# A two-layer fp32 decoder trunk on one core: x loaded ahead of the second weight strip, squares last, gated high parts queued behind the PSUM copies

## The chip, the cores and the metric

The kernel runs on one core of a Trainium2 chip, in one launch. The metric is the device time of that launch in microseconds (us). The kernel before was timed three times: 1942.38, 1941.19 and 1939.77 us, median 1941.19. One further execution was recorded by the profiler.

Engines are named as the profile names them: PE is TensorE (PEld its weight loads), DVE is VectorE, ACT is ScalarE, POOL is GpSimd, SP is the engine whose queue issues most transfers.

## The reference

The trunk works on a residual stream of 512 tokens by 1024 features in float32. It has two layers, each a half feed-forward, a mixer and another half feed-forward, so there are four feed-forward blocks, called ffn 0 to 3 here. The mixers (an mLSTM, a sparse attention) are not touched by the change.

```python
def rmsnorm(x, g):
    y = xf * lax.rsqrt(jnp.mean(xf * xf, axis=-1, keepdims=True) + EPS)
    return y * g

def swiglu(h, w_in, w_out):
    a, b = jnp.split(h @ w_in, 2, axis=-1)        # w_in: 1024 x 5632
    return (jax.nn.silu(a) * b) @ w_out           # w_out: 2816 x 1024

    h = h + 0.5 * swiglu(rmsnorm(h, ffn_norm[layer, 0]), ...)
```

## The kernel before

**Number format.** Every matrix product is made of three matmuls. An operand is cut into a high part (the value rounded to a shorter format) and a low part (value minus high part). ACT writes the high part with a copy, DVE subtracts it from the value and writes the low part. PE multiplies high by high, low by high and high by low into the same PSUM tile (`mm3`). Tile names tell which is which: `xhi`, `xlo` are the parts of the activations, `whi`, `wlo` of the weights, `thi`, `tlo` of sums of activations, `ghi`, `glo` of the gated hidden values.

**Layout.** The residual stream is held transposed, as eight tiles `h` of 128 features by 512 tokens. Weights come as strips of 128 output features, 512 KB each, through raw tiles `wraw` (two buffers), and are cut into `whi`, `wlo` (four buffers each). A strip against all of x is 8 times 3 matmuls of 512 columns.

**The start.** `setup` issues the loads on SP's queue: the first tile of x, the gains, three more tiles of x, the second weight strip as one 512 KB transfer (`load_weight`), the last four tiles of x, constants. The first strip was issued from ACT's queue in two halves (`load_first`). `norm_in` then makes the parts of x (ACT `xhi` line 289, DVE `xlo` line 290) and the sum of squares over the features: ACT squares a tile (lines 297 and 300), and POOL (tiles 1 to 3) or DVE (tiles 5 to 7) adds it to one of two sums `ssq` (line 301). The first two strips (p = 0) go through `plain`, which interleaves them: the second strip starts when the first has gone over four tiles of x. The next two strips (p = 1) follow. In them `rstd_columns` multiplies the sum of squares by a column of ones on PE and DVE computes the reciprocal root; `rstd_rows` later spreads it over the partitions with two matmuls from `rd`.

**A feed-forward block.** The 22 blocks of hidden features are taken in three thirds (`EVENS`: 8, 8 and 6 blocks). For a pair of blocks the gate half (weight block p) and the linear half (block 22 + p) are made, both mostly by `by_seven`: a two-by-two block product in seven instead of eight products, 84 matmuls of 256 columns. Its weights are quarters `q` and sums of quarters `s`, in four groups. The products land in three PSUM tiles A, Z and B. ACT copies quarters of them to SBUF in this order: A (into `fw`), the right half of Z (into `fu`), B (into `fu`), the rest of A (into `fw`), all on line 481. The fifth product writes the left half of Z, and is made to wait until ACT has copied Z's right half. After a gate half, `silu` multiplies by the reciprocal root on DVE (line 406) and applies SiLU on ACT (line 408). After a linear half, `gate` multiplies the two on DVE (line 415), and `split` writes `ghi` on ACT (line 245) and `glo` on DVE (line 246). At the end of a third, the gated blocks go through the out-projection. ffn 2 uses another variant (`by_seven_apart`).

**What sets the order.** A list scheduler merges the traced instructions into one queue for each engine. The engines work their queues strictly in order: an instruction that waits holds all that stand behind it on its engine.

Of the kernel before, what the change touches and what calls it, by code (L numbers as in the profile page):

```python
# [100 lines left out]
class Net:  # L101
# [38 lines left out]

    def load_weight(self):
# [107 lines left out]
    def setup(self):  # L249
# [6 lines left out]
        self.rest = lambda: None  # L256
# [20 lines left out]
    def norm_in(self, gcol, ssq=True, loaded=False):  # L277
# [7 lines left out]
        def parts(b):  # L285
            hi = self.xp.tile([P, T], F32R, name="xhi", tag="xhi")
            lo = self.xp.tile([P, T], F32R, name="xlo", tag="xlo")
            g = self.g[:, gcol + b:gcol + b + 1]
            nc.scalar.activation(hi, self.h[b], AF.Copy, scale=g)
            t = nc.vector.scalar_tensor_tensor(lo, self.h[b], g, hi.bitcast(F32), op0=ALU.mult, op1=ALU.subtract)  # L290
            self.part_made = t.ins
            x.append((hi, lo))

        def squares(b):
# [3 lines left out]
            else:  # L298
                sq = self.sp.tile([P, T], F32, name="sq", tag="sq", bufs=2)
                nc.scalar.activation(sq, self.h[b], AF.Square)  # L300
                (nc.gpsimd if b < 4 else nc.vector).tensor_tensor(t, t, sq, op=ALU.add)
# [7 lines left out]
        if ssq and loaded:  # L309
            for b in range(KB):  # L310
                squares(b)
# [65 lines left out]
    def ffn(self, i, given=None):  # L377
# [7 lines left out]
        with ExitStack() as ctx:  # L385
# [17 lines left out]
            def silu(pa):  # L403
# [4 lines left out]
                nc.scalar.activation(t, pa, AF.Silu)  # L408
                return t

            def gate(t, u):
# [5 lines left out]
                hi = gp.tile([P, T], F32R, name="ghi", tag="ghi", bufs=bufs)  # L417
                lo = gp.tile([P, T], F32R, name="glo", tag="glo", bufs=bufs)
                self.split(t, hi, lo)
                gs.append((hi, lo))  # L420
# [4 lines left out]
            def x_forms(k):  # L425
# [6 lines left out]
                nc.scalar.activation(one[:, :T], self.h[k], AF.Copy, scale=g1)  # L432
# [40 lines left out]
            def by_seven(p):  # L473
# [19 lines left out]
                out(u1[:, r], A[:, l])  # L493
# [48 lines left out]
            def plain(p):  # L542
# [7 lines left out]
                if p == 0:  # L550
                    order.sort(key=lambda o: o[0] + 3.5 * o[1])
# [22 lines left out]
            for k0, k1 in EVENS if seven else LATER:  # L574
# [5 lines left out]
                for p in range(k0, k1, 2) if seven or k0 else range(k0, k1):  # L580
                    if p and (seven or k0):
                        if p in units:
                            ts = [silu(t) for t in (yield from by_seven(p))]
                        else:
                            ts = []
                            for j in range(2):
# [12 lines left out]
                                ts.append(silu(pa))  # L599
                        for t, u in zip(ts, (yield from by_seven(FB + p))):  # L600
                            gate(t, u)
# [898 lines left out]
```

## Time and profile before

| what | value |
|---|---|
| median of 3 timed runs | 1941.19 us (1939.77 to 1942.38) |
| the profiled execution, its own time | 1940.4 us |
| its span, first to last instruction | 1938.6 us |
| mean granted clock of TensorE | 0.998 |
| POOL busy | 168.1 us (9% of the span) |
| bytes read from HBM | 177.10 MB, 92 GB/s over the span |

The span is the time from the first to the last instruction of the profiled execution; the 1.8 us to its own time lie outside. The other views used below are the timeline (start, duration, engine, line, operation, and in brackets the idle time before it with what ended it), the table of waits (who waited for whom: total, times, longest), and tables of time windows (busy time of each engine with the number of instructions, the clock granted to TensorE, and what the transfers moved).

### The profile page before, as it was taken

The numbers are of one execution on the slowest core, as the hardware profiler recorded it, in microseconds if no ns is written. First come the engines' busy times: TensorE is split into PE (matmuls) and PEld (weight loads), VectorE is DVE, ScalarE is ACT, GpSimd is POOL, SyncE is SP. The second block draws the span as 40 slices with busy tenths as digits, with TensorE's granted clock in tenths as the row PEclk, the third lists the DMA queues.
The fourth block names the chain that finished last, engine by engine and source line by source line (L and its number), as shares of the span: only waits on it lengthen the run. The fifth ranks groups of instructions, "written<-read, shape, count | busy, mean of one in ns | idle before, by whom it ended". The sixth has DMA issues, their size and how long they took to land. (4 is left out here: it accounts for less than half of the span.)

```text
span 1938.6 us, 31636 instructions
## 1 busy us (share of the span) xinstructions
PE 1913.0 (99%) x11946; PEld 1693.3 (87%) x11946; DVE 1567.4 (81%) x2947; ACT 1024.9 (53%) x1979; POOL 168.1 (9%) x222
## 2 busy tenths in 40 slices
PE   9999999999999999999999999999999999999999
PEld 7989898788878999898888989898877788999897
DVE  8969788757889879697676979696899989879695
ACT  6536345445656446265354535354777766445262
POOL 0000001012200000001100000001444410000000
PEclk9999999999999999999999999999999999999999
DMA  5333322323132323323343332323322222323322
GB/s 192 115 98 104 120 83 71 116 82 96 66 126 82 122 86 104 103 72 116 117 129 107 115 113 101 103 66 113 107 66 55 66 100 86 120 88 105 101 74 93
DMA packets 81945, 192.80 MB, mean 99 GB/s; under 512 B 9920, under 2 KB 10944, under 8 KB 81792
## 3 DMA queue, kind: packets, MB, share of 16 engines
q1 hardware_dynamic: 80272, 187.76, 30.3%
q8 instruction: 94, 1.54, 0.3%
q0 software_dynamic: 512, 1.31, 0.3%
q10 hardware_dynamic: 1008, 1.70, 0.2%
q14 instruction: 59, 0.48, 0.1%
HBM read 177.10 MB, written 2.10 MB: 92 GB/s over the span
## 5 line engine op out<-in xcount | busy, mean ns | idle before, releaser
L236 PE MATMUL pmm<-xhi,whi 128*128 128x256 f32 (+1 forms) x1376 | 441.4, 321 | 6.7 <-ACT fu L481 6.1
L236 PE MATMUL pmm<-xhi,wlo 128*128 128x256 f32 (+1 forms) x1376 | 437.5, 318 | 0.4 <-DVE wlo L170 0.4
L236 PE MATMUL pmm<-xlo,whi 128*128 128x256 f32 (+1 forms) x1376 | 437.0, 318 | 0.8 <-DVE xlo L290 0.8
L167 ACT ACTIVATE whi<-wraw 128x512 fp32r<-128x512 f32 (+3 forms) x258 | 204.8, 810 | 269.6 <-PE pmm L236 163.2
L236 PE MATMUL pmm<-thi,whi 128*128 128x256 f32 x1184 | 328.8, 278 | 2.4 <-ACT fw L516 2.0
L236 PE MATMUL pmm<-thi,wlo 128*128 128x256 f32 x1184 | 327.5, 277 | 1.4 <-DVE wlo L246 1.4
L236 PE MATMUL pmm<-tlo,whi 128*128 128x256 f32 x1184 | 327.7, 277 | 0.0
L170 DVE TENSOR_TENSOR wlo<-wraw,whi 128x512 fp32r<-128x512 f32 (+3 forms) x258 | 240.3, 944 | 70.6 <-ACT whi L167 67.8
L236 PEld LDWEIGHTS pmm<-xhi,whi 128*128 128x128 f32 x1376 | 258.4, 188 | 26.2 <-ACT fu L481 7.7
L236 PEld LDWEIGHTS pmm<-xhi,wlo 128*128 128x128 f32 x1376 | 258.4, 188 | 20.1 <-DVE wlo L170 0.7
L236 PEld LDWEIGHTS pmm<-xlo,whi 128*128 128x128 f32 x1376 | 258.6, 188 | 19.8 <-DVE xlo L290 2.6
L245 ACT ACTIVATE whi<-q 128x512 fp32r<-128x512 f32 x260 | 163.9, 631 | 209.1 <-PE pmm L236 156.1
L236 PE MATMUL pmm<-glo,whi 128*128 128x512 f32 x704 | 274.4, 390 | 0.0
L236 PE MATMUL pmm<-ghi,whi 128*128 128x512 f32 x704 | 274.2, 389 | 0.0
L236 PE MATMUL pmm<-ghi,wlo 128*128 128x512 f32 x704 | 273.9, 389 | 0.0
L236 PEld LDWEIGHTS pmm<-thi,whi 128*128 128x128 f32 x1184 | 223.2, 189 | 4.0 <-ACT fw L516 3.3
L236 PEld LDWEIGHTS pmm<-thi,wlo 128*128 128x128 f32 x1184 | 223.0, 188 | 1.6 <-DVE wlo L246 1.6
L236 PEld LDWEIGHTS pmm<-tlo,whi 128*128 128x128 f32 x1184 | 223.4, 189 | 0.0
L246 DVE TENSOR_TENSOR wlo<-q,whi 128x512 fp32r<-128x512 f32 x260 | 178.0, 685 | 16.4 <-ACT whi L245 16.4
L245 ACT ACTIVATE whi<-s 128x512 fp32r<-128x512 f32 x222 | 138.5, 624 | 54.6 <-PE pmm L236 32.7
L236 PEld LDWEIGHTS pmm<-glo,whi 128*128 128x128 f32 x704 | 132.2, 188 | 28.0 <-DVE glo L246 1.1
L236 PEld LDWEIGHTS pmm<-ghi,wlo 128*128 128x128 f32 x704 | 132.2, 188 | 27.6
(380 smaller groups left out, 3246.7 us busy)
## 6 DMA issues: line engine op xcount, KB each, us to landing
q<-in_ffn_in SPq DMA_DIRECT2D x260, 256.0 KB, 2.6
wraw<-in_ffn_out SPq DMA_DIRECT2D x48, 512.0 KB, 3.5
wraw<-in_ffn_out SPq DMA_DIRECT2D x48, 384.0 KB, 3.1
wraw<-in_ffn_in SPq DMA_DIRECT2D x27, 512.0 KB, 3.8
e<-in_ffn_in SPq DMA_DIRECT2D x36, 256.0 KB, 2.7
wraw<-in_m_qk SPq DMA_DIRECT2D x8, 512.0 KB, 3.6
wraw<-in_m_v SPq DMA_DIRECT2D x8, 512.0 KB, 3.6
wraw<-in_m_og SPq DMA_DIRECT2D x8, 512.0 KB, 3.6
```

The lines of the kernel that those rows point to most:

```text
L167: t = nc.scalar.activation(hi[:p, c], raw[:p, c], AF.Copy)
L170: nc.vector.tensor_tensor(lo[:p, c], raw[:p, c], hi[:p, c].bitcast(F32), op=ALU.subtract)
L236: self.nc.tensor.matmul(out, lhsT, rhs, start=start, stop=stop, skip_group_check=shared)
L245: self.nc.scalar.activation(hi, src, AF.Copy)
L246: self.nc.vector.tensor_tensor(lo, src, hi.bitcast(F32), op=ALU.subtract)
```

## The change

The changed kernel computes the same. It moves work on three engines in the start and in ffn 0, 1 and 3.

1. **Loads.** All eight tiles of x are issued ahead of the second strip, which is now loaded in two halves of 256 KB and cut into parts half by half (`load_second`). Its parts are traced after all parts of x.
2. **First product.** In ffn 0 the first strip goes over all eight tiles of x, and then the second strip does.
3. **Squares.** In ffn 0 all eight squares and their additions stand behind the parts of x and of the second strip on ACT and DVE, and all additions are on DVE.
4. **Parked parts.** In `by_seven` blocks of ffn 0, 1 and 3, SiLU and the split of the gated values are kept back, and traced behind the last of the next block's four PSUM copies (or, at a third's end, after the last block).

```diff
+    def load_second(self):
...
+        halves = slice(0, 512), slice(512, 1024)
+        for j, c in enumerate(halves):
+            nc.sync.dma_start(v(raw)[:, 4 * j:4 * j + 4], ap[:, 4 * j:4 * j + 4])
+        self.ready.append(((name, idx), (v(hi), v(lo))))
+        def parts():
+            for c in halves:
+                a = nc.scalar.activation(hi[:, c], raw[:, c], AF.Copy)
+                d = nc.vector.tensor_tensor(lo[:, c], raw[:, c], hi[:, c].bitcast(F32), op=ALU.subtract)
+            self.last = a.ins, d.ins
+        self.second = parts
...
         for b in range(KB):
             nc.sync.dma_start(self.h[b], a["xT"][b * P:(b + 1) * P, :])
...
-            if b == 3 and self.order:
-                self.load_weight()
+        if self.order:
+            self.load_second()
...
-                (nc.gpsimd if b < 4 else nc.vector).tensor_tensor(t, t, sq, op=ALU.add)
+                (nc.vector if b >= 4 or loaded else nc.gpsimd).tensor_tensor(t, t, sq, op=ALU.add)
...
         if ssq and loaded:
-            for b in range(KB):
-                squares(b)
+            self.second()
+            self.high_made, self.part_made = self.last
+            with self.tc.issue_after(self.high_made), self.tc.issue_after(self.part_made):
+                for b in range(KB):
+                    squares(b)
...
+            parked = deque()
+            def unpark():
+                while parked:
+                    parked.popleft()()
...
-                nc.scalar.activation(t, pa, AF.Silu)
+                if park:
+                    parked.append(lambda: nc.scalar.activation(t, t, AF.Silu))
+                else:
+                    nc.scalar.activation(t, pa, AF.Silu)
...
-                self.split(t, hi, lo)
-                gs.append((hi, lo))
+                def parts():
...
+                    self.split(t, hi, lo)
+                    gs.append((hi, lo))
+                if park:
+                    parked.append(parts)
+                else:
+                    parts()
...
                 yield from product(A[:, l], s2, -2, False)
-                out(u1[:, r], A[:, l])
+                with tc.issue_after(out(u1[:, r], A[:, l]).ins):
+                    unpark()
...
-                    order.sort(key=lambda o: o[0] + 3.5 * o[1])
+                    order.sort(key=lambda o: o[0] + (3.5 if i else 7.5) * o[1])
...
-                            ts = [silu(t) for t in (yield from by_seven(p))]
+                            ts = [silu(t, seven) for t in (yield from by_seven(p))]
...
-                            gate(t, u)
+                            gate(t, u, seven)
...
+                unpark()
                 n = k1 - k0
```

The next three places show queues as they were and as they are. A row has the line of its own kernel, the operation, what it writes and reads, and the size.

On ACT in the start, before, from the fourth tile of x on: squares (`ssq`, `sq`) and the second strip (`whi`, 1024 columns) stand between the parts of x.

```order
L289 ACTIVATE xhi<-h_73,gains 128x512
L297 ACTIVATE ssq_133<-h_70 128x512
L300 ACTIVATE sq<-h_71 128x512
L167 ACTIVATE whi<-wraw 128x1024
L289 ACTIVATE xhi<-h_74,gains 128x512
L289 ACTIVATE xhi<-h_75,gains 128x512
L300 ACTIVATE sq<-h_72 128x512
L289 ACTIVATE xhi<-h_76,gains 128x512
L289 ACTIVATE xhi<-h_77,gains 128x512
L300 ACTIVATE sq<-h_73 128x512
L297 ACTIVATE ssq_134<-h_74 128x512
L300 ACTIVATE sq<-h_75 128x512
```

The same queue in the changed kernel, from the last tile of x to the third and fourth strips (the last row, `whi` of 1024 columns, twice).

```order
L313 ACTIVATE xhi<-h_77,gains 128x512
L158 ACTIVATE whi<-wraw 128x512 x2
L321 ACTIVATE ssq_132<-h_70 128x512
L324 ACTIVATE sq<-h_71 128x512
L324 ACTIVATE sq<-h_72 128x512
L321 ACTIVATE ssq_133<-h_74 128x512
L324 ACTIVATE sq<-h_73 128x512
L324 ACTIVATE sq<-h_75 128x512
L476 ACTIVATE fw<-h_70,gains 128x512
L324 ACTIVATE sq<-h_76 128x512
L324 ACTIVATE sq<-h_77 128x512
L190 ACTIVATE whi<-wraw 128x1024 x2
```

All squares now stand between the second strip's parts and the third strip's.

On DVE in the start, before, from the second strip's low part to the third and fourth strips' (the last row): three additions of squares (`ssq`), the other three being POOL's.

```order
L170 TENSOR_TENSOR wlo<-wraw,whi 128x1024
L290 SCALAR_TENSOR_TENSOR xlo<-h_74,gains,xhi 128x512
L290 SCALAR_TENSOR_TENSOR xlo<-h_75,gains,xhi 128x512
L290 SCALAR_TENSOR_TENSOR xlo<-h_76,gains,xhi 128x512
L290 SCALAR_TENSOR_TENSOR xlo<-h_77,gains,xhi 128x512
L301 TENSOR_TENSOR ssq_134<-ssq_134,sq 128x512 x2
L197 TENSOR_TENSOR s_210<-q_194,q_196 128x512
L301 TENSOR_TENSOR ssq_134<-ssq_134,sq 128x512
L198 TENSOR_TENSOR s_211<-s_210,q_190 128x512
L313 TENSOR_TENSOR ssq_134<-ssq_134,ssq_133 128x512
L199 TENSOR_TENSOR q_194<-q_190,q_194 128x512
L170 TENSOR_TENSOR wlo<-wraw,whi 128x1024 x2
```

The same queue in the changed kernel, from the last tile of x to the low part of the fourth strip.

```order
L314 SCALAR_TENSOR_TENSOR xlo<-h_77,gains,xhi 128x512
L159 TENSOR_TENSOR wlo<-wraw,whi 128x512 x2
L325 TENSOR_TENSOR ssq_132<-ssq_132,sq 128x512 x3
L325 TENSOR_TENSOR ssq_133<-ssq_133,sq 128x512
L220 TENSOR_TENSOR s_213<-q_197,q_199 128x512
L325 TENSOR_TENSOR ssq_133<-ssq_133,sq 128x512
L221 TENSOR_TENSOR s_214<-s_213,q_193 128x512
L325 TENSOR_TENSOR ssq_133<-ssq_133,sq 128x512
L193 TENSOR_TENSOR wlo<-wraw,whi 128x1024
L340 TENSOR_TENSOR ssq_133<-ssq_133,ssq_132 128x512
L193 TENSOR_TENSOR wlo<-wraw,whi 128x1024
```

Six additions now stand between the second strip's low part and the third strip's, which has moved ahead of the last sum and of one sum of quarters.

On ACT in ffn 0, second third, at the gate half of block 14, before: the four PSUM copies are the rows with `pmm`; the two `ghi` are the gated values of blocks 12 and 13.

```order
L481 ACTIVATE fw<-pmm 128x256
L245 ACTIVATE ghi<-ft 128x512
L245 ACTIVATE whi<-q_2224 128x512
L245 ACTIVATE ghi<-ft 128x512
L481 ACTIVATE fu<-pmm 128x256
L245 ACTIVATE whi<-s_2359 128x512
L481 ACTIVATE fu<-pmm 128x256
L245 ACTIVATE whi<-q_2230 128x512
L481 ACTIVATE fw<-pmm 128x256
```

The same place in the changed kernel.

```order
L525 ACTIVATE fw<-pmm 128x256
L268 ACTIVATE whi<-q_2225 128x512
L525 ACTIVATE fu<-pmm 128x256
L268 ACTIVATE whi<-s_2354 128x512
L525 ACTIVATE fu<-pmm 128x256
L268 ACTIVATE whi<-q_2231 128x512
L525 ACTIVATE fw<-pmm 128x256
L268 ACTIVATE ghi<-ft 128x512 x2
L268 ACTIVATE whi<-s_2355 128x512
```

The two `ghi` have moved from behind the first copy to behind the fourth, and stand ahead of the high parts of later weights.

More of the change, by code (lines that the diff above doesn't have):

```diff
@@ L139, in load_first @@
         self.rest = lambda: self.split(raw[:, b], hi[:, b], lo[:, b])
+    def load_second(self):
+        nc = self.nc
+        name, idx = self.order.popleft()
+        ap = self.a[name][idx]
+        raw = self.wp.tile([P, 1024], F32, name="wraw", tag="wraw", bufs=2)
+        hi = self.part("whi")
+        lo = self.part("wlo")
+        v = lambda t: t.rearrange("p (n m) -> p n m", m=P)
+        halves = slice(0, 512), slice(512, 1024)
[8 more added lines that the diff above has]
+        self.second = parts
     def load_weight(self):
@@ L255, in setup @@
         nc.vector.memset(self.ones, 1.0)
-        self.rest = lambda: None
+        self.rest = self.second = lambda: None
+        self.last = None, None
         for b in range(KB):
@@ L288, in parts @@
             g = self.g[:, gcol + b:gcol + b + 1]
-            nc.scalar.activation(hi, self.h[b], AF.Copy, scale=g)
+            self.high_made = nc.scalar.activation(hi, self.h[b], AF.Copy, scale=g).ins
             t = nc.vector.scalar_tensor_tensor(lo, self.h[b], g, hi.bitcast(F32), op0=ALU.mult, op1=ALU.subtract)
@@ L407, in silu, with gate @@
                     pa = t
-                nc.scalar.activation(t, pa, AF.Silu)
+                if park:
+                    parked.append(lambda: nc.scalar.activation(t, t, AF.Silu))
+                else:
+                    nc.scalar.activation(t, pa, AF.Silu)
                 return t
-            def gate(t, u):
+            def gate(t, u, park=False):
                 if seven and not fold:
@@ L416, in gate @@
                 bufs = 8 if seven or not k0 else 6
-                hi = gp.tile([P, T], F32R, name="ghi", tag="ghi", bufs=bufs)
-                lo = gp.tile([P, T], F32R, name="glo", tag="glo", bufs=bufs)
-                self.split(t, hi, lo)
-                gs.append((hi, lo))
+                def parts():
+                    hi = gp.tile([P, T], F32R, name="ghi", tag="ghi", bufs=bufs)
+                    lo = gp.tile([P, T], F32R, name="glo", tag="glo", bufs=bufs)
+                    self.split(t, hi, lo)
[4 more added lines that the diff above has]
+                    parts()
             def gate_plain(pa, pb):
@@ L431, in x_forms @@
                 h2, c = self.h[k + 4], [two[:, N * j:N * j + N] for j in range(3)]
-                nc.scalar.activation(one[:, :T], self.h[k], AF.Copy, scale=g1)
+                with tc.issue_after(self.high_made):
+                    nc.scalar.activation(one[:, :T], self.h[k], AF.Copy, scale=g1)
                 with tc.issue_after(self.part_made):
```

4 lines of the change are left out of this document (2 added, 2 removed).

## The prediction, made before the changed kernel was run

> **What bounds the kernel now.** I read the page first, for the engine that bounds it.
>
> ```profile
> span 1938.6 us, 31636 instructions
> PE 1913.0 (99%) x11946; PEld 1693.3 (87%) x11946; DVE 1567.4 (81%) x2947; ACT 1024.9 (53%) x1979; POOL 168.1 (9%) x222
> ```
>
> PE is busy for 99% of the span, and the change removes no matmul. So the gain can only come from PE's idle time, 25.6 us by this row, and from time in which PE runs slowly. The table of waits says where PE's queue stands longest.
>
> ```profile
> PEld pmm L236 <- ACT fu L481: 7.7, 8, 2.2
> ```
>
> The first weight load after a wait is held 8 times, 7.7 us in all, by a PSUM copy (`fu`, line 481) on ACT. All lie in ffn 0, 1 and 3. The timeline shows one of them: block 14 of ffn 0.
>
> ```profile
> 195.56 0.38 ACT L481 ACTIVATE fw<-pmm 128x256 f32<-128x256 f32 x1 [0.78 <-PE pmm L236]
> 198.71 0.63 ACT L245 ACTIVATE ghi<-ft 128x512 fp32r<-128x512 f32 x1 [2.77 <-DVE ft L415]
> 200.29 0.36 ACT L481 ACTIVATE fu<-pmm 128x256 f32<-128x256 f32 x1
> ...
> 196.79 0.68 DVE L246 TENSOR_TENSOR wlo<-s,whi 128x512 fp32r<-128x512 f32 x1
> 198.60 0.68 DVE L415 TENSOR_TENSOR ft<-ft,fu 128x512 f32<-128x512 f32 x1
> 199.80 1.31 DVE L246 TENSOR_TENSOR glo<-ft,ghi 128x512 fp32r<-128x512 f32 x2
> ...
> 199.32 0.28 PE L236 MATMUL pmm<-thi,wlo 128*128 128x256 f32 x1
> 200.70 0.38 PE L236 MATMUL pmm<-xhi,whi 128*128 128x256 f32 x1 [1.10 <-ACT fu L481]
> 200.93 0.28 PE L236 MATMUL pmm<-xlo,whi 128*128 128x256 f32 x1
> 201.04 0.28 PE L236 MATMUL pmm<-xhi,wlo 128*128 128x256 f32 x1
> ```
>
> ACT has nothing wrong with its speed. Its first `ghi` stands for 2.77 us until DVE has multiplied the gate (line 415), and the copy that PE needs is queued behind it. The matmul that could have gone at 199.43 (199.32 plus the normal distance 0.11) goes at 200.70, 1.27 us late, and the next follows at a distance of 0.23 instead of 0.11: each such wait costs another 0.11.
>
> The second kind of loss is seen in a table of windows.
>
> ```profile
> 1080.07:1083.49 3.42, 1.76 (x12) 1.55 (x13) 3.42 (x7) 3.25 (x7) 0.00 (x0) 1.00 0.25 77
> 1083.49:1086.90 3.41, 3.41 (x18) 3.41 (x17) 3.41 (x6) 1.26 (x2) 0.00 (x0) 0.50 0.53 169
> 1783.22:1786.63 3.41, 1.48 (x13) 1.48 (x13) 3.41 (x6) 3.41 (x9) 0.00 (x0) 1.00 0.24 87
> 1786.63:1790.05 3.42, 3.42 (x19) 3.42 (x18) 3.42 (x7) 1.37 (x4) 0.00 (x0) 0.50 0.45 150
> ```
>
> Columns: length, busy time of PE, PEld, DVE, ACT, POOL, granted clock, share and rate of the transfers. Twice PE was busy for only half of a stretch of 3.41 us, and both times the next 3.41 us ran at clock 0.50, which costs 1.7 us each. The second follows the longest of the eight waits (2.2 us, in ffn 3); the first is in ffn 2, which the change leaves alone.
>
> **The change in the blocks (parked parts).** The new queue has both `ghi` behind the fourth copy. In the example the copies then wait only for PE's own products. What hides the parked work: the `ghi` are needed by the out-projection, which for this pair comes more than a block later, and the third's last pair is unparked at once. What is late next is a weight part: PE's next weights, the low part of the fifth product's, ended at 196.79 + 0.68 = 197.47, 2 us ahead of 199.43. The `glo` at 199.80 move behind low parts of weights on DVE, so those come 1.2 us earlier than now, about as much as PE comes earlier. No transfer is added; SP's queue has the same order there. So I take all eight waits as gone: 7.7 + 8 x 0.11 = 8.6 us, and the clock stretch of ffn 3, 1.7 us: **10.3 us**. From below, 4 us (the leads of the weights eat half of the waits, and the clock falls elsewhere); from above, 12 us (the shift of time also moves the ffn 2 waits over two stretches, and its half clock goes too).
>
> The Trainium skill, "TensorE: Matmul & The Clock Gate", section "Why this matters for your kernels", says to avoid idle gaps of more than about 3 us, and that one idle window brings half clock back. By that, the wait of 2.2 us would not have lowered the clock, and the stretch would stay: 8.6 us instead of 10.3. The two rows above speak against it, since 1.9 us of idle time within one stretch preceded half clock both times.
>
> **The change in the start.** These rows carry the sum.
>
> ```profile
> 6.10:12.40 6.30, 5.13 (x17) 2.79 (x18) 4.96 (x7) 6.03 (x11) 1.30 (x2) 1.00 1.04 396
> ...
> 7.76 0.73 ACT L289 ACTIVATE xhi<-h,gains 128x512 fp32r<-128x512 f32 x1
> 13.88 0.61 ACT L297 ACTIVATE ssq<-h 128x512 f32<-128x512 f32 x1
> 14.40 0.62 ACT L300 ACTIVATE sq<-h 128x512 f32<-128x512 f32 x1
> 17.86 1.99 ACT L167 ACTIVATE whi<-wraw 128x1024 fp32r<-128x1024 f32 x2
> ...
> 6.99 2.28 DVE L290 SCALAR_TENSOR_TENSOR xlo<-h,gains,xhi 128x512 fp32r<-128x512 f32 x3
> 11.89 4.80 DVE L290 SCALAR_TENSOR_TENSOR xlo<-h,gains,xhi 128x512 fp32r<-128x512 f32 x4
> 18.61 0.69 DVE L301 TENSOR_TENSOR ssq<-ssq,sq 128x512 f32<-128x512 f32 x1
> 21.02 2.36 DVE L170 TENSOR_TENSOR wlo<-wraw,whi 128x1024 fp32r<-128x1024 f32 x2
> ...
> 12.37 1.41 POOL L301 TENSOR_TENSOR ssq<-ssq,sq 128x512 f32<-128x512 f32 x1 [1.49 <-ACT sq L300]
> ...
> 6.13 0.47 PE L236 MATMUL pmm<-xhi,whi 128*128 128x512 f32 x1
> 10.53 0.50 PE L236 MATMUL pmm<-xhi,whi 128*128 128x512 f32 x1 [0.46 <-ACT whi L167]
> 12.02 0.50 PE L236 MATMUL pmm<-xhi,wlo 128*128 128x512 f32 x1 [0.38 <-DVE wlo L170]
> 20.52 0.39 PE L236 MATMUL pmm<-xhi,wlo 128*128 128x512 f32 x1
> 20.75 0.39 PE L236 MATMUL pmm<-xhi,whi 128*128 128x512 f32 x1
> 21.20 0.94 PE L236 MATMUL pmm<-ones,ssq 128*128 128x1 f32 x8
> 22.01 0.48 PE L236 MATMUL pmm<-xhi,whi 128*128 128x512 f32 x1
> 22.33 0.46 PE L236 MATMUL pmm<-xhi,wlo 128*128 128x512 f32 x1
> ```
>
> The first two strips are 48 matmuls at a distance of 0.23 (20.52 to 20.75), 10.9 us of work; they take 6.13 to 20.75, so 3.7 us are lost. Transfers run at 396 GB/s, 0.66 us for 256 KB. Step by step for the changed queues:
> 1. The fourth tile of x has landed when its `xhi` begins, 7.76. The other four now follow directly, the last at 10.4. With 0.73 on ACT and 0.75 on DVE the last `xlo` ends at 11.9. DVE no longer stretches: now four `xlo` take 4.80 us, 1.2 each, while POOL adds (12.37), against 0.76 each in the group of three. On SP's queue the second strip moves behind the four tiles and takes two issues for one, but as many bytes are in flight, so the quarters behind it land when they did. The fourth strip's load waits for the second raw buffer, free at 13.2 (step 2) instead of 12.0; its `whi` is due 5 us later. PE keeps pace, three matmuls of 0.23 for each `xlo` of about 0.68, and ends the first strip near 12.6.
> 2. The second strip's halves land at 11.1 and 11.7; DVE ends their low parts at 12.6 and 13.2, in time. 24 matmuls later, at 18.1, PE is through both strips: 2.6 us ahead of 20.75.
> 3. But the third strip's high part stands behind eight squares and one copy. ACT begins them at 12.35: 8 x 0.52 + 0.61 = 4.8, to 17.1; its `whi` ends at 18.1. DVE does six additions and two sums at 0.61 to 0.69 from 13.2 to 18.7 and the low part, 1.2, by 19.9. PE waits for it there, at its third matmul, where it now waits until 22.33. By 22.33 it has also done the eight passes with ones and one more matmul, 0.8 + 0.2. So the gain is 22.33 - 19.9 - 1.0 = **1.3 us**: half of step 2 is given back.
>
> One wait follows, for the reciprocal root's low part.
>
> ```profile
> 26.98 1.06 ACT L167 ACTIVATE whi<-wraw 128x1024 fp32r<-128x1024 f32 x1 [1.54 <-DMA wraw<-in_ffn_in]
> ...
> 36.03 0.40 PE L236 MATMUL pmm<-rd,unit 128*128 128x512 f32 x1
> 36.86 0.49 PE L236 MATMUL pmm<-rd,unit 128*128 128x512 f32 x1 [0.43 <-DVE rd L246]
> ```
>
> It costs 0.6 now. DVE's chain to `rd` starts earlier too: the fifth strip's load (awaited at 26.98) is issued when the third strip's low part frees its buffer, 2.4 us earlier (19.9 for 22.3). I take **0.3 us** more gain; between 0.7 (no wait) and a loss of 1.3 (the chain is no earlier and PE waits all of it). The start in sum: 1.6, between 0 and 3.3 (step 3 gives nothing back). POOL's additions in the other norms stay.
>
> **Sum.** 10.3 + 1.6 = 11.9 us off the profiled execution's 1940.4: **1928.5 us**. That execution lies 0.8 below the median of the timed runs, within their 2.6 us; I add nothing for it.
>
> **The rivals.**
> *DVE takes over.* A block of `by_seven` has 16 full operations on DVE (7 low parts, 4 sums, 2 combinations, 3 for gating) at 0.60 (two of them lie between 198.60 and 199.80), 9.6 us, against 84 x 0.113 = 9.5 on PE. DVE has no room to follow a faster PE, and PE would wait for `wlo` instead. For it: DVE stands without idle time around each wait. Against it: leads of 2 us, and this row of the out-projection, where DVE idles 18.8 us between thirds.
>
> ```profile
> 206.60:259.50 52.90, 52.90 (x276) 45.39 (x276) 34.14 (x48) 15.80 (x23) 0.00 (x0) 1.00 0.33 100
> ```
>
> If half of the 8.6 returns: 1928.5 + 4.3 = 1932.8. Chance 0.17.
> *The clock stretch stays.* If the half clock at 1786.63 has another cause than the wait ahead of it, it stays, or another takes its place (PE is idle for 1.3 us or more near 19, in one stretch): 1928.5 + 1.7 = 1930.2. Chance 0.12. The page named above has the rule that leads there.
> *The start gives nothing:* the squares hold the third strip until 21: 1930.1. Chance 0.10.
> *The parked parts hold the weights, and it is slower.* Both `ghi` now stand ahead of four `whi` of coming weights. If DVE's gate (line 415) ends more than 2 us after the fourth copy, PE waits in every pair. Each of the three ffn has 10 pairs. To end 4 us above, this must eat 11.9 + 4 = 16 us, 0.53 in each of 30 pairs: 1944.4 or more. The example's gate ends at 199.28, ahead of the fourth copy. Chance 0.03.
> *The change does not do what it says:* the copies stay behind. The order rows exclude it at the place shown; ends within 0.2% of before, with what else fails, get 0.08.
>
> **How the numbers follow.** The forecast has 0.50 (1926 to 1930.5), the others as given. The range reaches from 1925.5 (the ffn 2 clock stretch gone too, 1.7, and 1.3 of spread between runs) to 1936 (4 us from the blocks, next to nothing from the start). 0.2% of 1941.19 is 3.9 us, about what a measurement of this kernel can tell from no change, so faster means below 1937.3: 0.50 + 0.12 + 0.10, and 0.15 of DVE's: 0.87. Within: 0.09. Slower: 0.04.
>
> **What would show it.** Right: no row of PE waiting for ACT `fu` line 481 over 0.2 us; the matmul after 200.70's product begins within 0.2 of its predecessor; no clock of 0.50 in ffn 3; the 49th matmul of the start near 18.2, the third strip's low part ended near 19.9, PE idle 1.2 us there; `xlo` at 0.75 throughout. Wrong: PE waits for `wlo` line 269 inside thirds (DVE rival), a `glo` wait longer than now at the out-projections, a clock of 0.50 before 25 us, or a third strip later than 21.

## The result, and the profile after

| | before | changed |
|---|---|---|
| median, first chip | 1941.51 us (4 runs, 1939.77 to 1942.38) | 1930.47 us (4 runs, 1928.36 to 1934.27) |
| ratio, first chip | | 0.9946, 95% interval 0.9929 to 0.9964 |
| median, second chip | 1944.73 us (17 runs) | 1933.20 us (5 runs) |
| ratio, second chip | | 0.9937, 95% interval 0.9922 to 0.9952 |
| the profiled execution | 1940.4 us, span 1938.6 | 1928.36 us, span 1926.4 |

The changed kernel is 11 us faster, about 0.55%. The profiled execution came out at 1928.36 us (forecast 1928.5); the median of the four runs is 2 us above it. Of all executions timed for this text, one, with the start alone, ran at a granted clock of 0.71 and took 2494.38 us; it is left out of the numbers below. The page of the changed kernel:

```profile
span 1926.4 us, 31657 instructions
PE 1906.3 (99%) x11946; PEld 1688.9 (88%) x11946; DVE 1565.1 (81%) x2951; ACT 1030.3 (53%) x1980; POOL 165.1 (9%) x219
```

PE's idle time by these rows fell from 25.6 to 20.1 us, and its busy time by 6.7 us, though it has the same 11946 matmuls: a busy PE that runs slowly was part of what went. The table of waits of the changed kernel, PE's weight loads, from the top:

```profile
PEld po L259 <- DVE ptl L269: 4.0, 11, 0.6
PEld pmm L259 <- ACT fw L561: 3.4, 8, 0.8
```

The row that led this table before, ACT `fu` (line 481, now 525), is gone altogether. What is left on top lies in a mixer (`po`, `ptl`) and in ffn 2 (line 561). The timeline of block 14 of ffn 0, the place that the prediction showed:

```profile
193.10 0.38 ACT L525 ACTIVATE fw<-pmm 128x256 f32<-128x256 f32 x1 [0.79 <-PE pmm L259]
194.89 0.37 ACT L525 ACTIVATE fu<-pmm 128x256 f32<-128x256 f32 x1
...
197.61 0.37 ACT L525 ACTIVATE fw<-pmm 128x256 f32<-128x256 f32 x1
197.87 1.15 ACT L268 ACTIVATE ghi<-ft 128x512 fp32r<-128x512 f32 x2
...
195.51 0.68 DVE L451 TENSOR_TENSOR ft<-ft,fu 128x512 f32<-128x512 f32 x1
...
196.87 0.28 PE L259 MATMUL pmm<-thi,wlo 128*128 128x256 f32 x1
196.98 0.28 PE L259 MATMUL pmm<-xhi,whi 128*128 128x256 f32 x1
```

The copy `fu` now ends 1.8 us after the first copy ended (195.26 against 193.48), where it took 4.7 us before. The matmul of the fifth product (196.98) follows its predecessor at the normal 0.11. DVE's gate ends at 196.19, so the two `ghi` at 197.87 find it done.

The start, from three engines:

```profile
17.56 1.99 ACT L190 ACTIVATE whi<-wraw 128x1024 fp32r<-128x1024 f32 x2
...
7.03 4.24 DVE L314 SCALAR_TENSOR_TENSOR xlo<-h,gains,xhi 128x512 fp32r<-128x512 f32 x6
...
13.84 2.89 DVE L325 TENSOR_TENSOR ssq<-ssq,sq 128x512 f32<-128x512 f32 x4 [0.34 <-ACT sq L324]
...
19.06 1.22 DVE L193 TENSOR_TENSOR wlo<-wraw,whi 128x1024 fp32r<-128x1024 f32 x1
...
17.98 0.39 PE L259 MATMUL pmm<-xhi,wlo 128*128 128x512 f32 x1
18.65 0.50 PE L259 MATMUL pmm<-xhi,whi 128*128 128x512 f32 x1 [0.28 <-ACT whi L190]
20.33 0.50 PE L259 MATMUL pmm<-xhi,wlo 128*128 128x512 f32 x1 [0.94 <-DVE wlo L193]
```

Six `xlo` take 4.24 us, 0.71 each. PE has finished both strips at 18.2 (17.98 and a normal distance), and waits for the third strip's high part (0.28) and low part (0.94), which ends at 20.28.

Windows of ffn 2 and ffn 3 (length, busy PE, PEld, DVE, ACT, POOL, granted clock, share and rate of the transfers), at the places that had the half clock before:

```profile
1073.52:1076.93 3.41, 2.00 (x14) 1.80 (x15) 3.41 (x7) 3.13 (x7) 0.00 (x0) 1.00 0.23 79
1076.93:1080.35 3.42, 3.42 (x32) 3.42 (x31) 3.42 (x7) 1.18 (x3) 0.00 (x0) 1.00 0.61 203
1773.27:1776.69 3.42, 3.42 (x32) 3.42 (x32) 3.42 (x6) 2.51 (x7) 0.00 (x0) 1.00 0.26 81
```

No clock of 0.50 is left inside the work of this execution. In ffn 2 the waits are still there (PE is busy for 2.00 of 3.41 us), but by the grid of stretches of 3.41 us (experiment three) they fall so that only 1.41 us of idle time lie in one stretch, and no half clock followed.

Where the time went is best seen by the start times of the same matmul (counted in PE's order) in the two profiled executions:

| matmul | place | before | changed | difference | gained since the row above |
|---|---|---|---|---|---|
| 420 | end of the start | 71.90 | 70.41 | -1.5 | 1.5 |
| 2300 | behind ffn 0 | 348.18 | 343.37 | -4.8 | 3.3 |
| 4400 | in ffn 1, ahead of its first wait | 734.60 | 729.77 | -4.8 | 0.0 |
| 5500 | end of ffn 1 | 886.36 | 878.99 | -7.4 | 2.5 |
| 10700 | in ffn 3, ahead of its first wait | 1750.01 | 1742.25 | -7.8 | 0.4 |
| 11100 | ffn 3, second third | 1799.83 | 1787.59 | -12.2 | 4.5 |
| 11945 | last | 1934.77 | 1922.14 | -12.6 | 0.4 |

The start gave 1.5, and ffn 0, 1 and 3 gave 3.3 + 2.5 + 4.5 + 0.4 = 10.7.

### The profile page after: what moved, and what is told of

The parts are those of the page before. It is cut to its first block, busy times and chain, and to the rows that moved or that the text cites. A ratio compares the mean times of both kernels' runs of the same rounds, so it can differ in the third digit from the quotient of the medians.

```text
span 1926.4 us, 31657 instructions
## 1 busy us (share of the span) xinstructions
PE 1906.3 (99%) x11946; PEld 1688.9 (88%) x11946; DVE 1565.1 (81%) x2951; ACT 1030.3 (53%) x1980; POOL 165.1 (9%) x219
## 3 DMA queue, kind: packets, MB, share of 16 engines
q0 software_dynamic: 512, 1.31, 0.3%
## 4 chain that ended last, share of the span: by engine, by line
PE 87%; DVE 8%; ACT 3%; issue 1%; DMA 1%; POOL 0%; SPq 0%; DVEq 0%; ACTq 0%
PE pmm L259 78%; PE vps L259 2%; PE po L259 1%; PE S L259 1%; PE pt L1316 1%; DVE wlo L269 1%; DVE pr L1281 1%; PE paux L259 1%; DVE wlo L193 1%; PE pn L259 1%; ACT pr L1284 1%; DVE ptl L269 1%; DMA wraw<-in_ffn_in 0%; PE dm L259 0%; PE pt L259 0%
```

## The experiments

The theory that went into them: the eight waits for `fu` are ACT's `ghi` standing in front of the copies, worth 8.6 us; the half clock of ffn 3 is the result of the longest of these waits; the start's gain comes from x being loaded ahead and from the squares being last. Times of different chips are compared through the kernel before, which ran beside each.

### One: the parked parts alone, the start alone

The first kernel is the changed one with its edits of the start undone. The second leaves the parts unparked:

```diff
-                            ts = [silu(t, seven) for t in (yield from by_seven(p))]
+                            ts = [silu(t) for t in (yield from by_seven(p))]
...
-                                ts.append(silu(pa, seven))
+                                ts.append(silu(pa))
...
-                            gate(t, u, seven)
+                            gate(t, u)
```

> The parked parts alone, with the start of the kernel before. Theory: the eight waits for the copies are worth 8.6 us and the half-clock stretch of ffn 3 goes with its wait, 1.7: 1941.5 - 10.3 = 1931.2, no row of PE waiting for the copy `fu`, and no clock of 0.50 in ffn 3; the ffn 2 stretch may stay or go (its two waits stand at another place of the 3.41 us grid), so 1929.5 to 1931.5. Rival, DVE takes over: PE waits for low parts of weights inside thirds instead, 1934 or more. Rival, the changed kernel owes its missing half-clock stretches to the earlier start: then the one of ffn 3 stays here, 1932.9.

> The start alone, with nothing parked. Theory: matmul by matmul the changed kernel is 2.0 us ahead at 77 us, so 1941.5 - 2.0 = 1939.5; all eight waits for `fu` are there again, 7.5 to 8 us in sum, and the one of 2.2 us in ffn 3 is followed by 3.41 us at clock 0.50. Rival, the start gives nothing that lasts: 1941.5. Rival, the half clock depends on the time of day and not on the wait: the stretch of ffn 3 is gone here though the wait is there, 1937.8.

Measured on one chip, the kernel before at 1942.19 us (17 runs): the parked parts alone 1932.40 us, ratio 0.9950 (0.9938 to 0.9962); the start alone 1941.06 us (ten runs), ratio 0.9994 (0.9982 to 1.0006), which can't be told from no change. The top of the waits of PE's weight loads, first with the start alone:

```profile
PEld pmm L259 <- ACT fu L525: 8.3, 10, 2.7
```

With the parked parts alone the row is gone, and this one leads:

```profile
PEld pmm L259 <- ACT fw L557: 4.1, 8, 1.2
```

Matmul by matmul against before, the parked parts alone gain 3.4 us in ffn 0, 2.5 in ffn 1 and 4.5 in ffn 3. The start alone is 1.5 us ahead at matmul 420, as in the changed kernel (not 2.0, as expected), but only 0.4 at the end: 1.5 us were lost between 886 and 1079 us, where the edit touches nothing. By medians the two shares add up (9.8 and 1.1 us, against 11), but each is known to some 2 us only. The half clock of ffn 3 went with its wait: with the start alone the wait is 2.65 us, and the clock is 0.50 from 1784.34 to 1787.76 us; with the parked parts alone there is neither, and no clock of 0.50 inside the work. Of the DVE rival little is left: in ffn 3, at the out-projection near 1793 us (1790 in the changed kernel), PE's weight loads now wait 0.2 and 0.6 us for low parts of its weights (line 193), which they did not before. No wait for a low part stands where the eight waits were.

### Two: which of the two parked things counts

The edit of the first kernel is the first two pairs of the diff above (silu at its old place), that of the second is the last pair (high and low parts at their old place).

> The changed kernel with the high and low parts parked, and the silu at its old place. Theory: ahead of every one of the eight late copies stands a `ghi` that waited 1.1 to 3.7 us for the gate, and no silu; so this is the whole gain, the time of the changed kernel within 1 us, and no wait for `fu`. Rival, silu counts too: some of the waits return, 2 us or more.

> The changed kernel with the silu parked, and the high and low parts at their old place. Theory: all the waits for `fu` are back, 7 to 8.5 us in sum, and the time is that of the start alone, 1939 to 1941. Rival, silu counts: 3 us or more of them are gone.

Measured on the second chip (before 1944.73): with the high and low parts parked and the silu not, 1942.68 us, ratio 0.9996 (0.9985 to 1.0007): no gain clear of the noise. With the silu parked and the high and low parts not, 1930.52 us (one run, beside 1930.79 to 1934.81 of the changed kernel): the whole gain, and its trace has no wait for `fu`. Both expectations failed, in the same direction. The first kernel's waits and timeline show what stands in the way now:

```profile
PEld pmm L259 <- ACT fu L525: 8.3, 12, 1.3
PEld pmm L259 <- ACT ghi L268: 3.3, 3, 1.6
```

```profile
750.04 0.38 ACT L525 ACTIVATE fw<-pmm 128x256 f32<-128x256 f32 x1 [0.79 <-PE pmm L259]
753.16 1.29 ACT L444 ACTIVATE ft<-ft 128x512 f32<-128x512 f32 x2 [2.74 <-DVE ft L439]
754.36 0.37 ACT L525 ACTIVATE fu<-pmm 128x256 f32<-128x256 f32 x1
```

It is the silu of the gate half (`ft`, line 444), which waits 2.74 us for DVE's product (line 439) in front of the copy. The same holds for all twelve waits. The second row is a cost of its own: at the three out-projections that end ffn 0, 1 and 3, PE waits for a `ghi` that now comes late. In the kernel before the silus stood in the same places, and 24 of them waited for DVE (33.2 us), but ahead of seven of the eight late products stood a `ghi`. Only ahead of the eighth, the smallest (0.19 us), stood two silus, which the expectation had missed. With the silu alone parked, the `ghi` stand in front of the copy at block 14 as before, and wait only 1.50 us:

```profile
193.24 0.39 ACT L525 ACTIVATE fw<-pmm 128x256 f32<-128x256 f32 x1 [0.79 <-PE pmm L259]
195.12 1.24 ACT L268 ACTIVATE ghi<-ft 128x512 fp32r<-128x512 f32 x2 [1.50 <-DVE ft L451]
196.26 0.37 ACT L525 ACTIVATE fu<-pmm 128x256 f32<-128x256 f32 x1
```

The sums of ACT's waits in ffn 0, 1 and 3, and the time from the end of the first copy to the end of the second, over the 57 blocks of `by_seven`:

| kernel | silu waits for DVE (line 406/439) | `ghi` waits for the gate (line 415/451) | second copy behind the first: mean, longest |
|---|---|---|---|
| before | 24 times, 33.2 us | 27 times, 50.4 us | 2.76, 5.60 |
| high and low parts parked alone | 25 times, 52.3 us | 9 times, 20.6 us | 2.39, 4.68 |
| silu parked alone | once, 0.5 us | 26 times, 41.5 us | 1.93, 3.30 |
| changed | once, 0.5 us | 9 times, 25.7 us | 1.70, 1.77 |

At block 14 of the kernel before, the copy ended 4.7 us behind the first and PE lost 1.27, so PE puts up with some 3.4 us. The silu alone brings the longest case to 3.30, just inside. Both operations wait for the same thing, DVE's place in its queue; which of them holds a copy longer than 3.4 us depends on how far DVE is behind at that block. Why DVE is nearer to PE when the silu is parked (where the first of a pair's two gates ends behind the beginning of the first copy, it ends 1.66 us behind it on average over 22 blocks; before, 2.08 over 21) was not taken apart: the silu held up the high parts behind it on ACT, and so DVE's low parts, but no run isolates that.

### Three: how long must PE be idle for half clock

Behind the stores of the changed kernel, 40 groups of 46 matmuls were added, each released by one DVE operation of eight sizes in turn (`IDLE` holds the sizes; `one` is all zeros).

```diff
+            for rep in range(5):
+                for r, c in IDLE:
+                    v = lambda t: t[:, :r * c].rearrange("p (r c) -> p r c", c=c)
+                    nc.vector.tensor_tensor(v(w), v(one), ps[:, None, :c].to_broadcast([P, r, c]), op=ALU.mult)
+                    for n in range(46):
+                        self.mm(ps, w[:, :P], rhs, n == 0, n == 45)
```

> The changed kernel, and behind its stores forty groups of 46 matmuls 128x512 (10.4 us of work each), each group released by one DVE operation whose length goes through eight sizes five times, so that PE is idle for some 0.6 to 2.9 us between groups. Theory: half clock follows a stretch of the 3.41 us grid in which PE was idle for more than a bound between 1.1 and 1.7 us (the waits of the two kernels lie on both sides of these); so idle times under 1.1 us never lower the clock, those of 2.4 and more always do unless the grid cuts them in two, and each time the clock is 0.50 for exactly one stretch of 3.41 us. Rival, the rule of the Trainium skill (TensorE: Matmul & The Clock Gate): only idle times of more than about 3 us lower the clock, so none of these does.

One run, 2457.94 us. PE was idle for 0.38, 0.78, 1.18, 1.31, 1.65, 1.85, 2.11 and 2.58 us ahead of a group, five times each. None of the 25 idle times up to 1.65 us was followed by half clock; of 1.85, 2.11 and 2.58 us, 1, 3 and 2 of five were. The windows are set on the grid of 3.41 us that the half-clock stretches give; each pair is a stretch with an idle time and the one after it:

```profile
2002.58:2005.99 3.41, 1.76 (x9) 1.15 (x8) 1.55 (x1) 0.00 (x0) 0.00 (x0) 1.00 0.00 0
2005.99:2009.41 3.42, 3.42 (x16) 2.81 (x17) 0.00 (x0) 0.00 (x0) 0.00 (x0) 1.00 0.01 2
2016.23:2019.65 3.42, 1.57 (x7) 1.05 (x6) 1.75 (x1) 0.00 (x0) 0.00 (x0) 1.00 0.00 0
2019.65:2023.06 3.41, 3.41 (x9) 2.63 (x8) 0.00 (x0) 0.00 (x0) 0.00 (x0) 0.50 0.00 0
2326.85:2330.26 3.41, 1.51 (x7) 0.93 (x5) 1.87 (x1) 0.00 (x0) 0.00 (x0) 1.00 0.00 0
2330.26:2333.67 3.41, 3.20 (x14) 2.67 (x15) 0.16 (x1) 0.00 (x0) 0.00 (x0) 1.00 0.00 0
```

An idle time of 1.65 us in one stretch did nothing, 1.85 halved the next, and 1.90 (2.11 us, cut by the grid) did not. In the five stretches with 2.10 us or more inside, half clock always followed, for one stretch. Outside this probe, the work of the kernels before and changed and of the experiments has 13 stretches with 1.93 us or more of idle time, and half clock followed each of them. The bound lies near 1.9 us, a little over half of a stretch, above the 1.1 to 1.7 us expected. It is not sharp by the idle time that the trace shows: in the kernel before, and in two of the experiments, two waits of 1.64 to 1.66 us in sum within one stretch were enough, and in a third experiment they were not. The Trainium skill, "TensorE: Matmul & The Clock Gate", section "Why this matters for your kernels", warns of idle gaps of more than about 3 us. The measurement decides: here some 1.9 us were enough, and the place of the gap in the grid counts as well as its length: 2.58 us, cut in two by the grid, did nothing three times of five.

### Four: the pieces of the start

Three kernels each undo one piece of the start in the changed kernel: the additions of tiles 1 to 3 back on GpSimd, the weaving of the first two strips, and the second strip's load behind the fourth tile.

```diff
-                (nc.vector if b >= 4 or loaded else nc.gpsimd).tensor_tensor(t, t, sq, op=ALU.add)
+                (nc.gpsimd if b < 4 else nc.vector).tensor_tensor(t, t, sq, op=ALU.add)
```

```diff
-                    order.sort(key=lambda o: o[0] + (3.5 if i else 7.5) * o[1])
+                    order.sort(key=lambda o: o[0] + 3.5 * o[1])
```

```diff
-        if self.order:
-            self.load_second()
+            if b == 3 and self.order:
+                self.load_second()
```

> The changed kernel with the additions of the squares of tiles 1 to 3 on GpSimd, as before, at their new place behind the second strip. Theory: the `xlo` keep their 0.75 us, since the additions now begin behind them; each addition takes some 1.4 us, and the two `sq` buffers hold ACT's squares back for it, so the third strip's high part ends at 19.5 to 20 in place of 18.5 and its low part at 20.7 to 21.3 in place of 20.3: a loss of 0.4 to 1 us. DVE operations beside the additions take up to 1.2 us in place of 0.69. Rival, DVE is the bound here: three additions less on it bring the low part 1 us forward, a gain of 0.5 to 1 us.

> The changed kernel with the first two strips woven as in the kernel before (3.5 in place of 7.5). Theory: after the strips of four tiles, at about 8.8, PE wants the second strip, whose high part ends at 12.1: an idle time of 3 us in one piece, then 36 matmuls, done at 20.6; the 3.41 us stretch with the wait is followed by one at clock 0.50, 1.7 us more, 22.3. The third strip's low part, at 20.3, hides what lies before: a loss of 0.7 without and 2.4 us with the half clock. Rival, the order is worth nothing, since the third strip's low part sets the time anyway: within 0.3 us.

> The changed kernel with the second strip's load back behind the fourth tile of x, as in the kernel before; squares, additions and the order in the code stay as changed. The queues that come of it have the second strip's parts behind the fourth tile's on ACT and DVE, and PE goes to the second strip there. Theory: the same work of ACT and DVE stands ahead of the third strip's parts, so its low part ends at 20.3 again and PE gets to its third matmul there: within 0.5 us of the changed kernel, and the load order is worth nothing by itself. Rival: the last four tiles land 1.3 us later, their parts and the squares end later, the third strip's low part at 21.3 or later: a loss of 1 to 1.5 us, and with an idle time near 2 us on PE half clock and 1.7 us more.

The edit of the weaving (1931.11 us, ratio 0.9939, 0.9924 to 0.9955) and that of the load order (1934.67 us, ratio 0.9957, 0.9943 to 0.9971) change nothing in the start: at matmul 130, near 32 us, both stand within 0.2 us of the changed kernel on the second chip. My expectation for the weaving assumed that PE follows the order in the code. It doesn't: in this trace, as in the changed kernel's, the first strip goes over nearly all tiles before the second begins, and only a few matmuls stand differently. So this run does not test the order itself. With the load order undone, PE comes to the same wait (the brackets hold the idle time and what ended it):

```profile
20.92 0.50 PE L259 MATMUL pmm<-xhi,wlo 128*128 128x512 f32 x1 [1.19 <-DVE wlo L193]
```

Its first matmuls came 0.6 us later than in the first profile of the changed kernel, hence 20.92. The load-order kernel's profiled execution (1935.02 us) lost its time in ffn 2 (last section), not in the start; what made its median higher is not shown beyond that.

The additions on GpSimd (1935.21 us, ratio 0.9965, 0.9953 to 0.9978) cost far more than the 0.4 to 1 us expected: 5.6 us at matmul 130, against the changed kernel on the second chip. POOL, ACT and DVE, then the windows of the grid:

```profile
14.04 4.42 POOL L325 TENSOR_TENSOR ssq<-ssq,sq 128x512 f32<-128x512 f32 x3 [13.59 <-ACT sq L324]
...
17.11 0.63 ACT L324 ACTIVATE sq<-h 128x512 f32<-128x512 f32 x1 [1.12 <-POOL ssq L325]
19.57 1.99 ACT L190 ACTIVATE whi<-wraw 128x1024 fp32r<-128x1024 f32 x2
...
17.78 1.23 DVE L325 TENSOR_TENSOR ssq<-ssq,sq 128x512 f32<-128x512 f32 x1 [1.84 <-ACT sq L324]
```

```profile
17.40:20.81 3.41, 1.38 (x7) 0.84 (x6) 3.03 (x5) 3.28 (x6) 1.06 (x1) 1.00 0.69 249
20.81:24.22 3.41, 2.59 (x6) 1.58 (x7) 3.41 (x5) 0.75 (x1) 0.00 (x0) 0.50 0.20 41
24.22:27.64 3.42, 3.42 (x14) 3.04 (x13) 0.81 (x4) 0.00 (x0) 0.00 (x0) 0.50 0.84 259
27.64:31.05 3.41, 3.41 (x9) 2.64 (x9) 3.41 (x14) 3.03 (x5) 0.00 (x0) 0.50 0.03 12
31.05:34.46 3.41, 3.41 (x17) 2.82 (x16) 3.41 (x6) 2.51 (x5) 0.00 (x0) 1.00 0.53 155
```

The mechanism is the expected one, at twice the size: an addition takes 1.47 us on POOL (4.42 for three), ACT waits 0.36 and 1.12 us for a free `sq`, and the third strip's high part begins at 19.57 instead of 17.56. A DVE addition beside it takes 1.23 us, 0.68 without. The Trainium skill, "SBUF — State Buffer", section "Who interferes with whom", says that a DVE operation with two inputs in SBUF contends with a GpSimd one that reads SBUF; these rows agree. What the expectation had left out is the clock: PE is then idle for 2.03 us of one stretch, and three stretches at half clock follow. In the changed kernel the same waits, 0.28 and 0.94, stay below the bound.

### Five: bringing the third strip forward

Here the squares of the last two tiles, their additions and the sum move behind the third strip's parts, and the passes with ones two steps of three matmuls later.

```diff
-                for b in range(KB):
+                for b in range(6):
                     squares(b)
...
+            def late():
+                for b in (6, 7):
+                    squares(b)
+                t = nc.vector.tensor_tensor(acc[1], acc[1], acc[0], op=ALU.add)
...
+        if (name, idx) == ("ffn_in", (0, 1)):
+            with self.tc.issue_after(t.ins), self.tc.issue_after(d.ins):
+                self.late()
...
-                    if seven and p == 1 and t == 3:
+                    if seven and p == 1 and t == (3 if i else 5):
```

> The changed kernel with the squares of the last two tiles, their additions and the sum behind the third strip's parts, the quarters' sums behind these, and the eight passes with ones two strips later (sixth for fourth place). Theory: the 0.94 us wait for the third strip's low part and the 0.28 for its high part come from DVE and ACT doing squares first; the high part then begins when its transfer has landed, 16.3 to 16.6, the low part ends at 18.7 instead of 20.28, and 1.2 to 1.5 us are gained against the changed kernel: 1929.1. Rival: the sum ends at 21.7 and PE waits for it (passes due at 21.6) or for the reciprocal root at 35, 1 us or more, and nothing is gained: 1930.5.

Measured: 1933.94 us, ratio 0.9954 (0.9941 to 0.9967), no gain over the changed kernel. PE's timeline shows both halves:

```profile
18.73 0.50 PE L262 MATMUL pmm<-xhi,wlo 128*128 128x512 f32 x1
...
49.79 0.39 PE L262 MATMUL pmm<-xhi,wlo 128*128 128x256 f32 x1 [0.38 <-DVE wlo L272]
54.60 0.39 PE L262 MATMUL pmm<-thi,wlo 128*128 128x256 f32 x1 [0.42 <-DVE wlo L272]
94.18 0.50 PE L262 MATMUL pmm<-ghi,wlo 128*128 128x512 f32 x1 [1.19 <-DVE wlo L193]
```

The third strip's wait is gone (18.73 instead of 20.33), and at 32 us the kernel is 1.6 and 2.1 us ahead of the changed one's two profiles. Then PE waits for low parts of weights, and at 328 us it is 2.1 and 1.6 us behind them. The rival was right in kind but not in place: not the sum or the reciprocal root came late, but the low parts behind the work that was put off. In the changed kernel DVE is busy for 81 of the 83 us from 12 to 95 us; there, moving its work only moved PE's wait.

### Six: the same cause in ffn 2

ffn 2 has the same queue: a `ghi` in front of the copy `fw` of the first product. First its parts were parked too, and then the copy was also given another buffer.

```diff
-                            gate(t, u, seven)
+                            gate(t, u, True)
...
-                nc.scalar.activation(W[:, 0, :], X[:, :N], AF.Copy)
+                with tc.issue_after(nc.scalar.activation(W[:, 0, :], X[:, :N], AF.Copy).ins):
+                    unpark()
```

```diff
-                nc.scalar.activation(W[:, 0, :], X[:, :N], AF.Copy)
+                with tc.issue_after(nc.scalar.activation(U, X[:, :N], AF.Copy).ins):
+                    unpark()
...
-                TT(U, X[:, N:], W[:, 0, :], op=ALU.add)
+                TT(U, X[:, N:], U, op=ALU.add)
+                nc.scalar.activation(W[:, 0, :], X[:, :N], AF.Copy)
```

> The changed kernel with the gated parts parked in ffn 2 too, behind the copy `fw` of the first product. Theory: the same cause stands there, the first `ghi` ahead of the copy waits for DVE's gate, and the eight late products of the changed kernel (six by 0.19 to 0.8 us in what the timeline shows, 3 us with the restarts) go: 2.5 to 3 us less than the changed kernel, no row of PE waiting for ACT `fw` over 0.2 us. Rival, DVE is the bound in ffn 2: its gate and the coming low parts are no earlier, PE waits for `wlo` instead and under 1 us is gained.

> The changed kernel once more, on one chip with the next three. Theory: half clock follows a stretch of the 3.41 us grid with more than about 1.7 to 1.9 us of idle time on PE, and only the two waits of ffn 2 (0.7 and 1.4 us, 1.9 us apart) come near it, so an execution has none or one such stretch inside the work, by where the grid lies, at 1.7 us each: the runs at clock 1.000 stand 1 to 3 us below those at 0.999 and 0.998, and the median is 0.993 to 0.996 of the kernel before.

> The changed kernel with the gated parts of ffn 2 parked as before, and with the first product's copy made into `fq`, which is free by then, in place of `fw`, which DVE's gate still reads; `fw` gets its copy after the third product. Theory: in ffn 2 two things held the copy, the queue (the `ghi` ahead of it) and its buffer (the gate of the block before reads `fw`), and parking removed only the first; now both are gone, and the late third products of ffn 2, 2.9 us in sum in the changed kernel, go: 2.5 to 3 us less than the changed kernel, and no row of PE waiting for this copy over 0.2 us. Rival, DVE is the bound there: PE waits for low parts `wlo` or for the sums in place of the copy, under 1 us is gained.

Parked alone: 1930.75 us, ratio 0.9926 (0.9911 to 0.9941), beside 0.9937 (0.9922 to 0.9952) of the changed kernel on the same chip; too near to tell apart. In its trace the waits are not gone. The copy now stands first in ACT's queue and waits itself:

```profile
1182.52 0.38 ACT L561 ACTIVATE fw<-pmm 128x256 f32<-128x256 f32 x1 [3.95 <-DVE ft L451]
1182.80 1.14 ACT L268 ACTIVATE ghi<-ft 128x512 fp32r<-128x512 f32 x2
```

DVE's gate (line 451) still reads the only buffer `fw` of the block before. This row is an extreme one: DVE had itself lost 2.30 us to a late transfer (last section). At 1203.46 and 1295.12 us the copy waits 1.66 and 1.90 us for the same operation without that. So the queue was one of two holds at this place. With the copy into `fq`: 1928.43 us (1927.61 to 1930.64), ratio 0.9929 (0.9917 to 0.9942). One wait of PE for the copy is left over 0.2 us:

```profile
PE pmm L259 <- ACT fq L561: 0.3, 1, 0.3
```

From matmul 6480 to 8200, in ffn 2, it gains 1.2 us on the changed kernel's profile on the second chip and 1.9 on the first one's, not 2.5 to 3: waits of 0.25 and 0.22 us for `ghi` and `glo` appear at an out-projection (1220 to 1222 us), where the parked parts now come late, and its profile too has one half-clock stretch in ffn 2 (1075.87 us). It has the lowest median of all kernels run, but not the lowest ratio to the kernel before on its chip, and its interval overlaps that of the changed kernel: a gain over that kernel is not shown.

The changed kernel's runs on the second chip agree only in part with the expected 1 to 3 us: 1930.79 us at clock 1.000, 1930.91 at 0.999, 1933.20, 1933.38 and 1934.81 at 0.998. In its profile (0.999) the half clock of ffn 2 is back, behind the same two waits:

```profile
1074.11:1077.53 3.42, 1.43 (x10) 1.03 (x9) 3.39 (x7) 3.12 (x6) 0.00 (x0) 1.00 0.22 59
1077.53:1080.94 3.41, 3.41 (x19) 3.41 (x18) 3.41 (x7) 1.69 (x4) 0.00 (x0) 0.50 0.47 147
```

## Why the prediction was right, and where its reasons were not

**Blocks, 10.3 us: right in size.** All eight waits are gone, and in their place came only some 1 us of waits of PE's weight loads at out-projections; ffn 0, 1 and 3 gave 10.7 us. The bound from below (leads of the weights eat half) wasn't needed. The reason given was only half the story: the step says that the gain comes from both `ghi` going behind the fourth copy. Experiment two shows that this alone is worth nothing that can be measured, and that parking the silu, which the working did not price, is enough by itself. The `ghi` was what stood in front of the late copy; the cause was ACT waiting for a DVE that is behind, and ACT has two kinds of operations that do so.

**The half clock of ffn 3, 1.7 us: right here, but not a constant.** It went with its wait, as forecast (experiment one). By the rule of the Trainium skill that experiment three quotes it would have stayed. The rows that the forecast went by don't both have 1.9 us of idle time, as it says: the one of ffn 2 has 1.66 (3.42 less 1.76). And such a stretch depends on how the grid cuts the wait. Over 52 runs of the kernel before, the median is 1940.1 us in the 8 runs at clock 1.000, 1942.3 in the 12 at 0.999, 1943.0 in the 25 at 0.998, 1947.0 in the 5 at 0.997 and 1947.9 in the 2 at 0.996. The profiled execution of the changed kernel also lost the half clock of ffn 2, which the prediction kept (it stood in the upper bound); on the second chip it was back. Stretches of this kind can account for a part of the one run at 1934.27 us (clock 0.998), which left no trace. The 3 us between the other three, all at 1.000, they don't explain; so the 2 us between the forecast and the median are the spread of the executions, which the prediction put at 1.3, and whose cause stays open but for the transfer in the last section. That the profiled execution hit the forecast to 0.14 us is luck: it was the fastest of the four, and without the 1.7 us that the forecast had kept in ffn 2.

**The start, 1.6 us: right in sum (1.5), by terms that were off.** Step 1 and 2: `xlo` at 0.71 and both strips done at 18.2 (18.1 predicted). The 1.2 us each of step 1 are a mean: of the four `xlo`, the two beside an addition on POOL took 1.77 and 1.78 us, the other two 0.74. Step 3 failed in size: the low part ended at 20.28, not 19.9, since DVE's additions began at 13.84 and not 13.2, and PE waits 0.28 us for the high part too; the kernel is 0.8 us ahead at matmul 130, not 1.3. The wait for `rd` is gone entirely, 0.7 more instead of 0.3. The sum of 1.5 is also that of one pair of profiles: at matmul 420 the old start stands at 71.90 us in one profile and at 72.89 in the other (the parked parts alone), the new one between 70.36 and 70.94 in eight. Experiment four corrects the reasons: loading x ahead is worth nothing by itself in the start; what taking the first strip alone is worth is not shown, since no run undid it alone; the additions on GpSimd would cost 5 us at their new place.

**Rivals.** DVE as the new bound: not in the blocks, but true of the first 100 us (experiment five). The clock stretch that stays: not where its wait went. The start giving nothing: its gain shows at matmul 420 of every profile with the new start, but the timed runs of the start alone (0.9982 to 1.0006) don't show it. The parked parts holding the weights: not seen. No rival, and no term of the sum, had the silu in it.

## What to carry to other kernels

The operation in front of a late one is a symptom: ask what it waits for, and which other operations on that engine wait for the same; park each alone before saying which one counts. When a moved instruction still waits, look at its buffer: a queue and a buffer can hold it one behind the other. Where the engine that feeds PE has no idle time, moving its work moves PE's wait; what experiment four shows to last is keeping a slower engine out of its chain.

## What the runs showed of the hardware that was not expected

Half clock does not always last one stretch. With the additions on GpSimd three followed each other (10.24 us); PE was idle for 0.82 us of the first, and in the second most of its instructions were passes with ones of one column, though it counts as busy throughout. By these rows, what the clock counts is not quite the busy time of the profile.

One transfer in ffn 2 is sometimes slow. In 5 of 14 profiles a 256 KB quarter `e` took 4.4 to 5.0 us from issue to landing where the others took 2.6 to 3.1, and DVE stood for it:

```profile
1175.52 0.69 DVE L220 TENSOR_TENSOR s<-e,e 128x512 f32<-128x512 f32 x1 [2.30 <-DMA e<-in_ffn_in]
```

PE then waits 2.0 to 2.6 us near 1182 us, and half clock followed in four of the five, together about 4 us. Why that transfer is slow stays open. It is a part of the spread between runs of one kernel, as far as profiles were taken.
